# A decoder layer on one core: rows turned by DMA, the first two products in turn, weights laid out by the host

## Chip, core and metric

The kernel runs on one core of a Trainium2 chip. The metric is the device time of one launch in microseconds (us), the median over several runs. The core has five instruction streams that run side by side and wait for one another through semaphores: PE or TensorE (matrix products), DVE (VectorE), ACT (ScalarE), POOL (GpSimd) and SP (SyncE, which here only issues DMA transfers). ACT issues a few DMAs as well. The inputs lie in HBM, the working data in SBUF (128 partitions), and products accumulate in PSUM.

## What is computed

One layer of a hybrid decoder on 256 tokens of width 2048, in fp32, batch 1:

```python
hn = rmsnorm(h, norm_mix_w)
q, k, v, g_ret, xr, yr, g_a, g_b = split(hn @ w_in)
ret_out = silu(g_ret) * head_groupnorm(chunkwise_retention(rotary(q), rotary(k), v))
rnn_out = gelu(yr) * rg_lru(causal_dwconv(xr))
merged = sigmoid(g_a) * (ret_out @ w_proj_ret) + sigmoid(g_b) * (rnn_out @ w_proj_rnn)
h = h + merged @ w_mix_out
h = h + memory_cross_attention(rmsnorm(h), rmsnorm(mem), xa_w_q, xa_w_k, xa_w_v, xa_w_o)
h = h + conv_gated_ffn(rmsnorm(h), ffn_w_up, ffn_w_down)
out = rmsnorm(h, final_norm_w)
```

`mem` has 256 tokens as well. The weights are 2048 x 14336 (`w_in`), seven of 2048 x 2048, 2048 x 11264 (`ffn_w_up`) and 5632 x 2048 (`ffn_w_down`): nearly all of the 388 MB that are read.

## The kernel before

**Products.** Every large product is cut into blocks of 512 output columns (`BW`) and walks its inner dimension in chunks of four 128-row tiles (`KC`). A chunk's weights are a tile `raw` of 1 MB. For precision each weight is split into a rounded part `hi` (an ACT cast, L214) and a rest `lo` (a DVE subtraction, L215), and so is the other operand (tiles named `s`, `v`). A product is then three partial products, without the lo-by-lo term.

`gemm_n` (L279 to 281) leaves tokens on the partitions: three matmuls of 512 columns for each 128-row tile and each half of the tokens, 96 for a block of 16 tiles. `gemm_t` (L269) leaves features on the partitions: for each tile and each of four 128-column groups one matmul of 512 columns (both parts of `s` against `hi`) and one of 256 (the rounded part against `lo`), 64 pairs for a block.

**The stream of weights.** `plan` lists the products in order, `stream` their chunks. `prefetch` issues the load of a chunk on SP's queue and then the casts and subtractions; it runs two chunks ahead (`AHEAD`). There are three `raw` buffers and six half-chunk buffers each for `hi` and `lo`, so a cast waits until TensorE has read the half-chunk three chunks back. A weight chunk lies in HBM as 512 rows of the matrix, so each partition gets four rows of 2 KB.

**Order.** A scheduler orders each engine's instructions ahead of time; each engine then runs its own list in that order. `later(n, fn)` puts work `n + 1` chunks behind the current one.

**Rows that must be turned.** The result of `gemm_n` has tokens on the partitions, but the next product needs features there. `transposed` (L309) turns 128 x 128 squares on TensorE, against the identity `cid`, into PSUM tiles `sm`, four squares in a group. It is used for the heads' outputs (`rc`), for the merged rows (`m`, `turn_merged`), and for the residual rows after `w_mix_out` and after `xa_w_o` (`nat`, `turn`). A turned pair is split into parts by `split_pair` or `split_cols` (ACT, then DVE; L330, L353, L354). For the block that ends last the product behind it is already running: its last chunk of rows needs the turned pairs.

**Start.** The first product is Q's first block. Its pieces of `w_in` and of the transposed input `x_t` are issued in turn on SP (`Pairs`, `xs`), then V's first block, then K's. The row sums of squares of x (`rms`, L429) are eight ACT instructions in one go, on tiles `nat` loaded on ACT's queue; they give a scale per token, `rs0`. `spread_tokens` lays such a scale out along the free dimension: a diagonal on DVE (L379) and two products with ones (L380), then an ACT copy into `rsb`.

**Memory attention.** `xa_w_k` works on the memory tokens, whose pairs `ms` are split from loads `xt<-in_mem_t` on the way; two of the eight are made ahead.

Of the kernel before, what the change touches and what calls it, by code (L numbers as in the profile page):

```python
# [11 lines left out]
I32 = mybir.dt.int32  # L12
AF = mybir.ActivationFunctionType
# [3 lines left out]
P = 128  # L17
# [20 lines left out]
FF_PARTS = [4, 4, 3]  # L38

# [23 lines left out]

@with_exitstack
def hybrid_layer(
# [5 lines left out]
    w_in: bass.AP,  # L71
    rg_w_a: bass.AP,
    rg_w_x: bass.AP,
    w_proj_ret: bass.AP,
    w_proj_rnn: bass.AP,
    w_mix_out: bass.AP,
    xa_w_q: bass.AP,
    xa_w_k: bass.AP,
    xa_w_v: bass.AP,
    xa_w_o: bass.AP,  # L80
    ffn_w_up: bass.AP,
    ffn_w_down: bass.AP,
    final_norm_w: bass.AP,
    consts: bass.AP,
# [64 lines left out]
    w0 = w_in[0]  # L149
    plan = []  # L150
    for g in range(2):
        for c in (O_Q, O_K):
            plan += [(w0, 0, NT, c + g * BW), (w0, 0, NT, O_V + g * 1024 + (c == O_K) * BW)]
        plan += [(w0, 0, NT, O_G + g * 1024 + b * BW) for b in range(2)]
    for b in range(4):
        plan += [(w0, 0, NT, c + b * BW) for c in (O_XR, O_YR)]
    for c, w in ((O_GB, w_proj_rnn[0]), (O_GA, w_proj_ret[0])):
        for b in range(4):
            plan += [(w0, 0, NT, c + b * BW), (w, 0, NT, b * BW)]
    plan += [(w_mix_out[0], 0, NT, b * BW) for b in range(4)]  # L160
    plan += [(w, 0, NT, b * BW) for b in range(4) for w in (xa_w_k[0], xa_w_q[0])]
    plan += [(w, 0, NT, b * BW) for w in (xa_w_v[0], xa_w_o[0]) for b in range(4)]
    b0 = 0
    for nb_ in FF_PARTS:
        for b in range(b0, b0 + nb_):
            plan += [(ffn_w_up[0], 0, NT, c + b * BW) for c in (0, FF)]
        plan += [(ffn_w_down[0], b0 * BW, 4 * nb_, b * BW) for b in range(4)]
        b0 += nb_
    stream = [(w, row + k * P, c) for w, row, nk, c in plan for k in range(0, nk, KC)]
# [11 lines left out]

    def prefetch(n):
        while len(ahead) < n and taken[0] < len(stream):
            w, row, c = stream[taken[0]]
            taken[0] += 1
            raw = wp.tile([P, KC, BW], F32, tag="raw", bufs=RAW_BUFS, name=nm("raw"))
            src = w[row : row + KC * P, c : c + BW].rearrange("(k p) n -> p k n", p=P)
            first = taken[0] == 1
            if taken[0] <= 4:
                xs.load(2 * taken[0] - 1)  # L190
            for a, b in ((0, 1), (1, 2), (2, 4)) if first else ((0, 2), (2, 4)) if taken[0] <= 3 else ((0, 4),):
                sp.dma_start(out=raw[:, a:b, :], in_=src[:, a:b, :])
                if first and a == 0:
                    sp.dma_start(out=xs.rest[0], in_=xs.rest[1])
                elif first and a == 1 or a == 0 and taken[0] <= 4:
                    xs.load(2 * taken[0])
            if taken[0] == 5:
# [3 lines left out]
            if taken[0] == 7:  # L201
                sp.dma_start(out=pf.rearrange("p a n -> p (a n)"), in_=by_feature[:, P + 80 :])
            parts = []
            for k in range(0, KC, KH):
                if taken[0] <= 4:
                    xs[2 * (taken[0] - 1) + k // KH]
                hi = wp.tile([P, KH, BW], F32R, tag="hi", bufs=PART_BUFS, name=nm("hi"))
                lo = wp.tile([P, KH, BW], F32R, tag="lo", bufs=PART_BUFS, name=nm("lo"))
                for cs in (slice(k, k + 1), slice(k + 1, k + 2)) if first and k == 0 else (slice(k, k + KH),):
                    ds = slice(cs.start - k, cs.stop - k)  # L210
                    if first and k == 0:
                        dve.tensor_copy(hi[:, ds], raw[:, cs, :])
                    else:
                        act.copy(hi[:, ds], raw[:, cs, :])  # L214
                    dve.tensor_tensor(  # L215
                        out=lo[:, ds], in0=raw[:, cs, :], in1=hi[:, ds].bitcast(F32), op=ALU.subtract
                    )
                parts.append((hi, lo))
            ahead.append(((row, c), parts))
            if taken[0] >= 4:  # L220
                load_x(min(4, 2 * (taken[0] - 3)))
# [7 lines left out]
    def chunks(nk, w, row, c):  # L229

        w_, row_, nk_, c_ = plan[gemms[0]]
        assert (row_, nk_, c_) == (row, nk, c) and w_.tensor is w.tensor, (gemms[0], row, nk, c)
        gemms[0] += 1
        for k in range(0, nk, KC):
# [4 lines left out]
            yield k, parts  # L239
# [6 lines left out]
    def gemm_t(w, row, st, nk, col):  # L246
# [4 lines left out]
        for k0, parts in chunks(nk, w, row, col):  # L251
            last = k0 + KC >= nk
            tiles = [(kk, j) for j in range(2) for kk in range(KC)]
            if first and k0 == 0:
                runs = [[(t, pr, kk, j) for t in (0, 1)] for pr in range(2) for kk in range(KC) for j in range(2)]
# [5 lines left out]
            for i, run in enumerate(runs):  # L261
# [10 lines left out]
                if i + 1 == len(runs) // 2 and not last:  # L272
                    st[(k0 + KC) // 2 + 1]
        return accs
# [8 lines left out]
    def gemm_n(w, row, st, nk, col):  # L283

        a = acc()
        for k0, parts in chunks(nk, w, row, col):
            for tt in range(2):
                for kk in range(KC):
# [3 lines left out]
        return a  # L292
# [10 lines left out]
    def transposed(rows):  # L303

        for k in range(0, rows.shape[2], 2 * P):
# [6 lines left out]
            yield t  # L312

# [59 lines left out]

    def spread_tokens(r):

        diag = tmp("diag")
        bc = small((P, S))
        for tt in range(2):
            dve.tensor_scalar_mul(diag[:, 0, tt * P : (tt + 1) * P], ident, r[:, tt : tt + 1])  # L379
            pe.matmul(  # L380
                bc[:, tt * P : (tt + 1) * P], ones, diag[:, 0, tt * P : (tt + 1) * P], start=True, stop=True
            )
        act.copy(rsb, bc)
# [9 lines left out]
    class Pairs(list):  # L393
        def __init__(self, src, wcol):
            self.src, self.wcol, self.raw = src, wcol, []
# [14 lines left out]
        def __getitem__(self, i):  # L410
            while len(self) <= i:
                k2 = len(self)
                self.load(min(NT // 2, k2 + 2))
# [3 lines left out]
    xs = Pairs(x_t, p_mix)  # L417
    qjoin = [joined(t, "q") for t in gemm_t(w0, 0, xs, NT, O_Q)]
# [4 lines left out]
    def rms(rows, pin=False):  # L423

        ss = sp_.tile([P, 2, 4], F32, tag="ss0", name=nm("ss"))
        for c in range(4):
            for tt in range(2):
                junk = tp.tile([P, BW], F32, tag="tmp", name=nm("junk"))
                i = act.activation(junk, rows[c][:, tt, :], AF.Square, accum_out=ss[:, tt, c : c + 1])  # L429
                if pin:  # L430
                    tc.keep_in_program_order(i)
        var = sp_.tile([P, 2], F32, tag="var", name=nm("var"))
        dve.tensor_reduce(out=var, in_=ss, axis=AX.X, op=ALU.add)
        return rsqrt_small(var, 2, 1.0 / D, EPS)

    rs0 = rms(xin, pin=True)
    dve.tensor_scalar_mul(half_rs0, rs0, 0.5)
    rsb = cp.tile([P, S], F32, name="rsb")
# [19 lines left out]
    def tables():  # L458
        spread_tokens(rs0)
# [16 lines left out]
    later(1, tables)  # L476
# [81 lines left out]
    for g in range(2):  # L558
        dec = big([P, 4, S], s="dec")
        vs, turned = [], []  # L560
        for b, o in enumerate((O_Q, O_K)):
            a = qjoin if g == b == 0 else [joined(t, "q") for t in gemm_t(w0, 0, xs, NT, o + g * BW)]
            if b == 0:
# [6 lines left out]
            v = gemm_n(w0, 0, xs, NT, O_V + g * 1024 + b * BW)  # L570
# [5 lines left out]
        for b in range(2):  # L576
            a = gemm_n(w0, 0, xs, NT, O_G + g * 1024 + b * BW)
# [71 lines left out]
    for b in range(4):  # L649
# [4 lines left out]
        for pr, a in enumerate(gemm_t(w0, 0, xs, NT, O_XR + b * BW)):  # L654
# [11 lines left out]
        for pr, a in enumerate(gemm_t(w0, 0, xs, NT, O_YR + b * BW)):  # L666
# [12 lines left out]
    def gated(c0, w, st, b, o):  # L679

        a = gemm_n(w0, 0, xs, NT, c0 + b * BW)
# [13 lines left out]
    mb = [gated(O_GB, w_proj_rnn[0], rnn, b, big([P, 2, BW], s="mb")) for b in range(4)]  # L695
    for b in range(4):
        m = gated(O_GA, w_proj_ret[0], ret, b, big([P, 2, BW], s="m"))
# [7 lines left out]
    ms = Pairs(mem_t, p_mem)  # L705

    def residual(w, st, out, wcol, steps=None):

        ss = sp_.tile([P, 2, 4], F32, tag="ss0", name=nm("ss"))
        for b in range(4):  # L710
# [9 lines left out]
    def turn(b, pr, out, wcol):  # L720
        for t in transposed(hrow[b][:, :, pr * S : (pr + 1) * S]):
            out.append(split_cols(t, lambda j: wcol(4 * b + 2 * pr + j)))
# [9 lines left out]
    def rstd_rows(ss):  # L732
        var = sp_.tile([P, 2], F32, tag="var", name=nm("var"))
        dve.tensor_reduce(out=var, in_=ss, axis=AX.X, op=ALU.add)
        return rsqrt_small(var, 2, 1.0 / D, EPS)

    rsms = []

    def memory_steps(b):
        if b == 1:  # L740
            rsms.append(rms(mnat))
            later(3, lambda: spread_tokens(rsms[0]))
# [6 lines left out]
    ss1 = residual(w_mix_out[0], merged, h1s, p_xa, memory_steps)  # L749
# [41 lines left out]
    for b in range(XH):  # L791
        ks = []
        for a in gemm_t(xa_w_k[0], 0, ms, NT, b * BW):
# [159 lines left out]
```

## Time and profile before

| | us |
|---|---|
| median of 3 runs (2048.63 to 2052.51) | 2050.64 |
| the profiled execution | 2048.89 |
| its span, first to last instruction | 2047.1 |
| TensorE busy / DVE / ACT | 2035.0 / 1309.3 / 1045.3 |
| weight loads of 1 MB, issue to landing, median | 4.9 to 5.1 |

The span is what the profile sees of the execution; the rest of the 2048.89 lies around it. Busy time is the union of an engine's instructions. Matmuls are pipelined, so a single one shows 0.39 us in the timeline while the next one starts 0.23 us after it; what a piece of work costs TensorE is read from the starts. In a timeline row the columns are the start, the duration, engine, line, operation, tiles (out<-in), shape and count, and in brackets the idle time of the engine before it and what ended that. In a row of groups the count is followed by busy time and mean duration in ns, then by the idle time before them. In a row of waits stand the total, the number of times and the longest. A row of DMA issues ends with the size of one and the median time from issue to landing.

### The profile page before, as it was taken

The numbers are of one execution on the slowest core, as the hardware profiler recorded it, in microseconds if no ns is written. First come the engines' busy times: TensorE is split into PE (matmuls) and PEld (weight loads), VectorE is DVE, ScalarE is ACT, GpSimd is POOL, SyncE is SP. The second block draws the span as 40 slices with busy tenths as digits, with TensorE's granted clock in tenths as the row PEclk, the third lists the DMA queues.
The fourth block names the chain that finished last, engine by engine and source line by source line (L and its number), as shares of the span: only waits on it lengthen the run. The fifth ranks groups of instructions, "written<-read, shape, count | busy, mean of one in ns | idle before, by whom it ended". The sixth has DMA issues, their size and how long they took to land.

```text
span 2047.1 us, 26196 instructions
## 1 busy us (share of the span) xinstructions
PE 2035.0 (99%) x10508; PEld 1746.4 (85%) x10508; DVE 1309.3 (64%) x1630; ACT 1045.3 (51%) x1357; POOL 7.7 (0%) x12
## 2 busy tenths in 40 slices
PE   9999999999999999999999999999999999999998
PEld 7888888888888888888888888888888888888887
DVE  6858758888444544566555555577764777656774
ACT  6545447677434444555444544455543555435553
POOL 0000000000000000000000000000000000000000
PEclk9999999999999999999999999999999999999999
DMA  9664554555655555766555555555555555655563
GB/s 327 210 211 152 199 191 160 175 178 180 209 187 196 192 185 190 261 210 211 176 178 176 174 173 176 179 180 198 193 185 205 184 188 185 202 189 182 189 216 114
DMA packets 200682, 392.25 MB, mean 192 GB/s; under 512 B 7024, under 2 KB 11760, under 8 KB 200560
## 3 DMA queue, kind: packets, MB, share of 16 engines
q1 hardware_dynamic: 199040, 387.95, 55.7%
q10 hardware_dynamic: 1520, 2.63, 0.4%
q8 instruction: 82, 1.34, 0.3%
q14 instruction: 40, 0.33, 0.0%
HBM read 388.46 MB, written 2.10 MB: 191 GB/s over the span
## 4 chain that ended last, share of the span: by engine, by line
PE 79%; DVE 0%; ACT 0%; issue 0%; POOLq 0%; DVEq 0%
PE acc L269 35%; PE acc L280 14%; PE acc L281 14%; PE acc L279 14%; PE sm L297 1%; PE sm L309 1%; PE sm L623 0%; DVE xr L640 0%; PE sm L783 0%; ACT hi L214 0%; ACT nat L878 0%; DVE lo L215 0%; ACT c L319 0%; PE sm L380 0%; ACT s L330 0%
## 5 line engine op out<-in xcount | busy, mean ns | idle before, releaser
L215 DVE TENSOR_TENSOR lo<-raw,hi 128x1024 fp32r<-128x1024 f32 (+1 forms) x713 | 860.3, 1222 | 608.4 <-ACT hi L214 562.4
L214 ACT CAST hi<-raw 128x1024 fp32r<-128x1024 f32 x711 | 736.2, 1052 | 718.3 <-PE acc L280 455.0
L269 PE MATMUL acc<-s,hi 128*128 128x512 f32 x2688 | 639.0, 391 | 2.5 <-ACT hi L214 1.9
L279 PE MATMUL acc<-hi,s 128*128 128x512 f32 (+1 forms) x1528 | 591.9, 387 | 0.0
L281 PE MATMUL acc<-lo,s 128*128 128x512 f32 (+1 forms) x1528 | 590.1, 386 | 0.0
L280 PE MATMUL acc<-hi,s 128*128 128x512 f32 (+1 forms) x1528 | 590.0, 386 | 0.0
L269 PEld LDWEIGHTS acc<-s,hi 128*128 128x128 f32 x2688 | 496.5, 188 | 101.7 <-ACT hi L214 2.7
L269 PEld LDWEIGHTS acc<-s,lo 128*128 128x128 f32 x2688 | 342.7, 191 | 11.8 <-DVE lo L215 1.1
L269 PE MATMUL acc<-s,lo 128*128 128x256 f32 x2688 | 350.4, 283 | 0.5 <-DVE lo L215 0.5
L281 PEld LDWEIGHTS acc<-lo,s 128*128 128x128 f32 x1528 | 287.1, 188 | 57.9
L280 PEld LDWEIGHTS acc<-hi,s 128*128 128x128 f32 x1528 | 287.2, 188 | 57.1 <-DVE s L331 0.4
L279 PEld LDWEIGHTS acc<-hi,s 128*128 128x128 f32 x1528 | 287.2, 188 | 56.6
L319 ACT COPY c<-acc 128x512 f32<-128x512 f32 x84 | 48.6, 581 | 111.8 <-PE acc L269 111.8
L320 DVE TENSOR_TENSOR uz<-acc,c 128x512 f32<-128x512 f32 x44 | 30.3, 688 | 27.4 <-ACT c L319 27.4
L835 DVE SCALAR_TENSOR_TENSOR fg<-uz,pf,fg 128x255 f32<-128x255 f32 (+1 forms) x88 | 39.2, 479 | 0.0
L835 DVE SCALAR_TENSOR_TENSOR fv<-uz,pf,fv 128x255 f32<-128x255 f32 (+1 forms) x88 | 38.4, 480 | 0.0
L353 ACT ACTIVATE s<-sm,pb 128x256 fp32r<-128x256 f32 x48 | 21.9, 471 | 17.7 <-DVE s L354 16.7
L443 DVE TENSOR_TENSOR uz<-uz,rsb 128x512 f32<-128x512 f32 x44 | 30.3, 689 | 0.7
L330 ACT ACTIVATE s<-fo 128x512 fp32r<-128x512 f32 x22 | 13.9, 632 | 26.7 <-DVE fo L904 26.7
L833 ACT ACTIVATE fv<-uz,pf 128x256 f32<-128x256 f32 x44 | 25.3, 600 | 2.5 <-DVE uz L443 2.5
L354 DVE SCALAR_TENSOR_TENSOR s<-sm,pb,s 128x256 fp32r<-128x256 f32 x48 | 22.4, 481 | 5.1 <-ACT s L353 5.1
L833 ACT ACTIVATE fg<-uz,pf 128x256 f32<-128x256 f32 x44 | 25.3, 599 | 0.0
(167 smaller groups left out, 731.0 us busy)
## 6 DMA issues: line engine op xcount, KB each, us to landing
raw<-in_w_in SPq DMA_DIRECT2D x109, 1024.0 KB, 5.0
raw<-in_ffn_w_up SPq DMA_DIRECT2D x88, 1024.0 KB, 4.9
raw<-in_ffn_w_down SPq DMA_DIRECT2D x44, 1024.0 KB, 5.1
raw<-in_w_proj_rnn SPq DMA_DIRECT2D x16, 1024.0 KB, 5.1
raw<-in_w_proj_ret SPq DMA_DIRECT2D x16, 1024.0 KB, 5.1
raw<-in_w_mix_out SPq DMA_DIRECT2D x16, 1024.0 KB, 5.1
raw<-in_xa_w_k SPq DMA_DIRECT2D x16, 1024.0 KB, 5.1
raw<-in_xa_w_q SPq DMA_DIRECT2D x16, 1024.0 KB, 5.1
```

Of the source, the lines that this page charges most:

```text
L214: act.copy(hi[:, ds], raw[:, cs, :])
L215: dve.tensor_tensor(out=lo[:, ds], in0=raw[:, cs, :], in1=hi[:, ds].bitcast(F32), op=ALU.subtract)
L269: pe.matmul(a, part, sx, start=k == 0 and t == 0, stop=k == nk - 1 and t == 0, skip_group_check=True)
L279: pe.matmul(o, h, hi, start=start, stop=False)
L280: pe.matmul(o, l, hi, start=False, stop=False)
L281: pe.matmul(o, h, lo, start=False, stop=stop)
L319: act.copy(c, a[:, :, S:BW])
L320: dve.tensor_tensor(out=o, in0=a[:, :, 0:S], in1=c, op=ALU.add)
L354: dve.scalar_tensor_tensor(out=t[:, j, S:BW], in0=src[:, j, :], scalar=wcol(j), in1=t[:, j, 0:S].bitcast(F32), op0=ALU.mult, op1=ALU.subtract,
L443: dve.tensor_tensor(out=z, in0=z, in1=rsb2, op=ALU.mult)
L833: act.activation(y, z[:, j, :], AF.Identity, scale=pf[:, 2, t : t + 1], bias=pf[:, 3, t : t + 1])
L835: dve.scalar_tensor_tensor(out=y[:, s:S], in0=z[:, j, 0 : S - s], scalar=pf[:, 2 - s, t : t + 1], in1=y[:, s:S], op0=ALU.mult, op1=ALU.add,)
```

## The change

There are five edits.

1. The merged rows and the residual rows are no longer turned on TensorE. ACT copies a block of rows into two planes of 16-bit halves, SP issues two transposing DMAs, one for each half of the tokens, and two chunks later ACT joins the halves into a tile `f`, which is split as before. The heads' outputs and the attention's probabilities are still turned on TensorE.
2. Q's first block and V's first block are computed in turn, in pieces of 2, 2, 4, 4 and 4 tiles.
3. All weights are handed over in one array `wall`, laid out by the host in the order of the stream, so that each partition of a chunk reads one row of 8 KB.
4. The eight squares of x are made as two groups of four, each ahead of the casts of one later chunk.
5. `spread_tokens` builds the diagonal at once and returns a function for the products and the copy.

```diff
+EARLY = [2, 2, 4, 4, 4]
...
+def weight_stream():
+    out = [
+        [(w, row + k * P, n, c) for k, n in pieces(i, nk)]
+        for i, (w, row, nk, c) in enumerate(weight_plan())
+    ]
+    out[:2] = [[one for pair in zip(*out[:2]) for one in pair]]
+    return [one for chunks in out for one in chunks]
...
+def weights_in_order(inputs):
+    out = []
+    for name, row, n, c in weight_stream():
+        w = np.asarray(inputs[name])[0][row : row + n * P, c : c + BW].reshape(n, P, BW)
+        out.append(w.transpose(1, 0, 2).reshape(-1))
+    return np.concatenate(out)
...
-            w, row, c = stream[taken[0]]
+            i = taken[0]
+            name, row, nk, c = stream[i]
             taken[0] += 1
+            size = nk * P * BW
+            src = wall[at[0] : at[0] + size].rearrange("(p k n) -> p k n", p=P, k=nk)
...
+            if i in (8, 9):
+                for b in (2 * i - 16, 2 * i - 15):
+                    sum_squares(xin[b], ss0, b, pin=True)
...
+    def by_dma(rows, then):
+        planes = big([P, 2, 2, BW], U16, s="pl")
+        turned_ = big([P, 2, 4, S], U16, s="pt")
+        words = rows.bitcast(U16).rearrange("p t (n h) -> p h t n", h=2)
+        for h in range(2):
+            act.copy(planes[:, :, h, :], words[:, h])
+        for tt in range(2):
+            sp.dma_start_transpose(
+                out=turned_.rearrange("p h f s -> p (h f) s")[:, :, tt * P : (tt + 1) * P],
+                in_=planes[:, tt].rearrange("p h n -> p (h n)"),
+            )
+        def join():
+            f = big([P, 4, S], s="f")
+            halves_ = f.bitcast(U16).rearrange("p f (s h) -> p h f s", h=2)
+            for h in range(2):
+                act.copy(halves_[:, h], turned_[:, h])
+            then(f)
+        later(1, join)
...
     def spread_tokens(r):
-        diag = tmp("diag")
-        bc = small((P, S))
+        diag = tp.tile([P, S], F32, tag="tr", bufs=2, name=nm("diag"))
         for tt in range(2):
-            dve.tensor_scalar_mul(diag[:, 0, tt * P : (tt + 1) * P], ident, r[:, tt : tt + 1])
-            pe.matmul(
-                bc[:, tt * P : (tt + 1) * P], ones, diag[:, 0, tt * P : (tt + 1) * P], start=True, stop=True
-            )
-        act.copy(rsb, bc)
+            dve.tensor_scalar_mul(diag[:, tt * P : (tt + 1) * P], ident, r[:, tt : tt + 1])
+        def products():
+            bc = small((P, S))
+            for tt in range(2):
+                cs = slice(tt * P, (tt + 1) * P)
+                pe.matmul(bc[:, cs], ones, diag[:, cs], start=True, stop=True)
+            act.copy(rsb, bc)
+        return products
...
-    xs = Pairs(x_t, p_mix)
-    qjoin = [joined(t, "q") for t in gemm_t(w0, 0, xs, NT, O_Q)]
+    xs = Pairs(x_t, p_mix, 1)
+    q_steps = steps_t("w_in", 0, xs, NT, O_Q)
+    v_steps = steps_n("w_in", 0, xs, NT, O_V)
+    for _ in EARLY[1:]:
+        next(q_steps)
+        next(v_steps)
...
-    def turn_merged(m, pr):
-        for t in transposed(m[:, :, pr * S : (pr + 1) * S]):
-            merged.append(split_pair(t, 0.5))
+    def turn_merged(f):
+        for pr in range(2):
+            merged.append(split_pair(f[:, 2 * pr : 2 * pr + 2, :], 0.5))
...
         dve.tensor_add(m, m, mb[b])
-        for pr in range(2):
-            later(pr, lambda m=m, pr=pr: turn_merged(m, pr))
+        by_dma(m, turn_merged)
...
             squares(h, ss, b)
-            for pr in range(2):
-                later(pr, lambda b=b, pr=pr: turn(b, pr, out, wcol))
+            by_dma(hrow[b], lambda f, b=b: turn(f, b, out, wcol))
```

`steps_t` and `steps_n` are `gemm_t` and `gemm_n` written as generators that stop after each chunk; `gemm_t` and `gemm_n` now run them to the end.

More of the change, by code (lines that the diff above doesn't have):

```diff
@@ L70, in hybrid_layer @@
     positions: bass.AP,
-    w_in: bass.AP,
     rg_w_a: bass.AP,
     rg_w_x: bass.AP,
[L74 to L82, printed above, removed]
     final_norm_w: bass.AP,
+    wall: bass.AP,
     consts: bass.AP,
@@ L146, in hybrid_layer @@
         pe.matmul(warm[:, 0, 0:P], ones, ones, start=True, stop=True)
[L149 to L169, printed above, removed]
+    plan = weight_plan()
+    stream = weight_stream()
     ahead, taken, gemms = [], [0], [0]
@@ L244, in chunks, with ended, steps_t @@
                 fn()
-    def gemm_t(w, row, st, nk, col):
+    def ended(steps):
+        for a in steps:
+            pass
+        return a
+    def steps_t(w, row, st, nk, col):
         accs = [acc(), acc()]
@@ L271, in gemm_t @@
                     )
-                if i + 1 == len(runs) // 2 and not last:
-                    st[(k0 + KC) // 2 + 1]
-        return accs
+                if i + 1 == len(runs) // 2 and not last and not first and isinstance(st, Pairs):
+                    st[(k0 + n) // 2 + 1]
+            yield accs
+    def gemm_t(*args):
+        return ended(steps_t(*args))
     def products_n(o, sx, hi, lo, tt, start, stop):
@@ L474, in tables @@
         dve.tensor_tensor(out=cos, in0=cos, in1=rsb, op=ALU.mult)
-    later(1, tables)
+    qjoin = [joined(t, "q") for t in next(q_steps)]
+    assert next(q_steps, None) is None
+    later(0, tables)
     def rotated(qs_):
@@ L792, in hybrid_layer @@
         ks = []
-        for a in gemm_t(xa_w_k[0], 0, ms, NT, b * BW):
+        for a in gemm_t("xa_w_k", 0, ms, NT, b * BW):
             z = joined(a, "kz")
```

187 lines of the change are left out of this document (109 added, 78 removed).

## The prediction

> **What bounds the kernel.** I read the page's busy times first, then the list of waits on TensorE.
>
> ```profile
> span 2047.1 us, 26196 instructions
> ...
> PE 2035.0 (99%) x10508; PEld 1746.4 (85%) x10508; DVE 1309.3 (64%) x1630; ACT 1045.3 (51%) x1357; POOL 7.7 (0%) x12
> ```
> ```profile
> PE acc L269 <- ACT hi L214: 1.9, 1, 1.9
> PE warm L146 <- DVE mhalf L141: 1.1, 1, 1.1
> PE sm L380 <- DVE diag L379: 0.6, 1, 0.6
> ```
>
> TensorE is idle for 12 us of 2047: before the first product, for two or three waits, and behind the last matmul (2039.4, so 7.7 us). Only two things can shorten this: less TensorE work, or a better start. Faster weights, DVE or ACT give nothing. Next the timeline of TensorE around one group of turning transposes, and the group rows:
>
> ```profile
> 887.01 0.39 PE L281 MATMUL acc<-lo,s 128*128 128x512 f32 x1
> 887.24 0.60 PE L309 MATMUL sm<-cid,nat 128*128 128x128 f32 x4
> 887.59 0.48 PE L279 MATMUL acc<-hi,s 128*128 128x512 f32 x1
> 887.91 0.40 PE L280 MATMUL acc<-hi,s 128*128 128x512 f32 x1
> 888.14 0.40 PE L281 MATMUL acc<-lo,s 128*128 128x512 f32 x1
> ```
> ```profile
> L309 PE MATMUL sm<-cid,nat 128*128 128x128 f32 x64 | 9.6, 272 | 0.0
> L309 PE MATMUL sm<-cid,m 128*128 128x128 f32 x32 | 4.8, 272 | 0.0
> ```
>
> Matmuls start every 0.227 us (512 wide) or 0.120 (256 wide). L281 at 887.01 should be followed by the next L281 at 887.69; it starts at 888.14. So four transposes cost 0.45 us.
>
> **The change, part by part.**
>
> *Transposes off TensorE.* 32 of `m` and 64 of `nat` are 24 groups: 24 x 0.45 = 10.8 us less on the path. The other transposes stay, and nothing is added to TensorE.
>
> *Start.* Timelines of TensorE and ACT:
>
> ```profile
> 8.07 0.91 ACT L353 ACTIVATE s<-xt,pa 128x256 fp32r<-128x256 f32 x2 [3.36 <-DMA xt<-in_x_t]
> 9.42 1.05 ACT L214 CAST hi<-raw 128x1024 fp32r<-128x1024 f32 x1 [0.44 <-DMA raw<-in_w_in]
> 10.52 0.74 PE L269 MATMUL acc<-s,hi 128*128 128x512 f32 x2 [1.95 <-ACT hi L214]
> 11.78 0.39 PE L269 MATMUL acc<-s,lo 128*128 128x256 f32 x1 [0.53 <-DVE lo L215]
> ```
>
> Q's first product runs from 4.75 to 30.94 (first L279), 26.2 us; its 64 pairs at 0.347 are 22.2: 4.0 lost, waiting for DMA, which by stretches of 2 us is full from 8 us on (374 to 404 GB/s). By queue order 1024 KB had landed at 8.05 and 1536 KB at 9.4. In the change the first piece of V lies within the first 1024 KB, so V starts at 8.05 + 0.5 (half an ACT cast) = 8.6 instead of standing until 10.52. V's first 12 matmuls take 2.7, to 11.3; the next Q piece closes 2048 KB, 10.8 at 385 GB/s, cast by 11.8. After that two k-blocks of Q and V need 1.25 MB per 5.5 us, 233 GB/s. Lost: 8.6 - 7.5 + 0.5 = 1.6, gain 2.4; bounds 0 (no better) and 4.0 (all).
>
> *Token scales.* The diagonal is built ahead of its two products, and the eight squares stand as two groups of four ahead of the casts of two later chunks. The L380 wait goes, 0.71 us with its sequencer time. The groups (four at 0.63 each) wait for `nat`, issued on ACT's queue and 8 to 13 us on the way, so there by about 29 and 36; the casts behind them are for products at 39 and 45. If that cover goes, each late us is a us.
>
> *Host-laid weights.* One 8 KB row per partition instead of four of 2 KB. Zero: a 1 MB load lands in 5.0 us, a chunk takes TensorE 5.45, and three buffers run ahead. If the cover went, it could only be a gain.
>
> *The DMA turn.* Per block of 512 columns: two ACT copies to 16-bit planes, two transposing DMAs of 256 KB on SP, two ACT copies back. Copies: nearest row 1.05 us for 128x1024, lower bound 0.58 (128x512 f32), upper 2.1 (two passes); I take 1.05. ACT gains 12 x 4.2 = 50 us of work and is half idle. No row has a transposing DMA. Call X the time from the last plane copy to the landing of both DMAs. The rows:
>
> ```profile
> out<-nat SPq DMA_DIRECT2D x6, 256.0 KB, 2.3
> ...
> cid<-in_consts SPq DMA_DIRECT2D x1, 65.0 KB, 8.3
> pa<-in_by_feature SPq DMA_DIRECT2D x1, 56.0 KB, 8.0
> pb<-in_by_feature SPq DMA_DIRECT2D x1, 40.0 KB, 7.5
> pa<-in_by_feature ACTq DMA_DIRECT2D x1, 8.0 KB, 2.5
> ```
>
> Lowest: two 2.3 us transfers issued 0.45 apart, 2.8. `cid`, `pa`, `pb` were issued at 16.18, 16.73, 17.48, so landed at 24.5, 24.7, 25.0: 128 small rows add 0.22 to 0.24 us whatever their length (320 to 520 B), 27.5 ns for each row on one of 16 engines. The source is read by runs of 128 two-byte elements, 2048 runs of 256 B: 128 x 27.5 ns = 3.5, plus issue 0.9, plus landing 2.3: X = 7. If the destination is written in runs of 16 elements (16384), 28 + 3: X = 31. If sixteen 128x128 squares go one after another, each a lone 2.5 us transfer: X = 39.5. I take 7: both sides have long contiguous runs.
>
> What waits: SP stands at the turn until the planes are made, with the next weight load behind it; that load's buffer comes free within about 2 us of the same moment, so nothing. ACT stands at the join copy, with the hi casts of the coming chunks behind it, and TensorE behind those. With T the end of the product that made the rows, planes end at T+7.3 for `m` (one hi cast goes first, its buffer free at T+4.1) and T+5.3 for the residual rows (add 1.2, squares 1.3, planes 2.1). The casts behind the join are mostly for the product at T+21.8 (96 x 0.227). Counting back casts, splits (0.45 and 0.6) and the join's 2.1, no stall while X is under: `m` blocks 0 to 2: 12; block 3: 12.7 (TensorE does a chunk and a bit of the next block first); `w_mix_out` rows 0 to 2: 18, 17, 10; `xa_w_o` rows 0 to 2: 14; row 3: 8, since the FFN wants it at T+16.4.
>
> One place stalls anyway, after the last `w_mix_out` block:
>
> ```profile
> 927.58 1.05 ACT L214 CAST hi<-raw 128x1024 fp32r<-128x1024 f32 x1 [0.61 <-PE acc L281]
> 929.39 0.63 ACT L730 ACTIVATE junk<-nat 128x512 f32<-128x512 f32 x1 [0.76 <-DVE nat L714]
> ...
> 932.58 0.91 ACT L353 ACTIVATE s<-xt,pb 128x256 fp32r<-128x256 f32 x2
> ```
>
> `xa_w_k`'s second chunk needs memory pairs (`s<-xt,pb`) at T+5.45 (two transposes' worth later here). With planes and one cast ahead of them they come at T+6.35 to 8.15: 1.9 us late. The last two pairs stand behind the join: 0.9 more at X = 7, and each us of X beyond 7 is a us. I add 2.8.
>
> Sum: -10.8 - 2.4 - 0.7 + 2.8 = -11.1: span 2036.0. The profiled execution took 2048.9, 1.8 over its span; the median of the runs is 2050.6. **Forecast 2050.6 - 11.1 = 2039.5.** Own range: all of the start and no late pairs, 2035; no start gain and copies at 2.1 (about 2 more at that place and the FFN row), 2044; with 2 us of spread between runs, 2033 to 2046.
>
> **Rivals.**
>
> *The turn is a little late*, X of 10 to 14 (transposes queue behind a weight load in flight, 5.0 us). At 12: 5 at the memory pairs, 4 at row 3 of `xa_w_o`, 2 at row 2 of `w_mix_out`: +11, so 2050.5, no change. For: those loads are on the same queue. Against: the load just ahead of the turn is issued some 5 us before it.
>
> *The turn is late everywhere; slower.* Mechanism: small runs, ACT held at the join. It decides from X = 12. At X = 31: 3x19 + 18 + 13 + 14 + 21 + 24 + 3x17 + 23 = 221, time 2260. For: the cost per small row above. Against: it needs both sides cut to 32 B.
>
> *Squares one after another; slower.* At X = 39.5 the same sum is 323: 2363. Against: plain DMAs overlap over 16 engines (share 1.05). By the Trainium skill, page "VectorE: DVE Perf Modes", section "The three transpose paths", a 128x128 two-byte transpose takes 1309 ns by DMA against 390 ns on TensorE; sixteen in a row would make X 20.9, stalls 100 and the time 2140, an estimate from that page. The trace prices TensorE's at 0.45/4 = 0.11 us for fp32, so the page's comparison does not settle this one; no run here yet shows the DMA's.
>
> *It does less than it says:* the start is bound by the first 1.5 MB whatever the order, 2042; inside my range.
>
> **Chances.** Forecast 0.62 (2033 to 2046); a little late 0.12 (2046 to 2056); late everywhere 0.13; one after another 0.08; another stall of a few us in a product whose order on ACT I have not priced 0.05. A measurement of this kernel tells 0.2% from no change, about 4 us. Faster 0.64, within 0.2% 0.09, slower 0.27. 2031 to 2060 holds the first two, most of the last and the near end of the late ones.
>
> **What would show it.** Right: no `cid,m` and `cid,nat` transposes; TensorE starting V near 8.6; join copies on ACT with no idle time ended by the DMA beyond 3 us; TensorE idle in all about 12 to 14 us. Wrong: TensorE waits on `hi` spread over the gated, `w_mix_out` and `xa_w_o` stages (X too large); landings of the turned planes over 12 us; plane copies far from 1.05 us; a wait at `xa_w_k` that is absent or far over 3 us.

## The result, and the profile after

The changed kernel took 2039.24 us (median of 4 runs, 2038.36 to 2042.19), the kernel before 2050.58 (4 runs beside it, 2048.63 to 2052.51): ratio 0.9951, 95% interval 0.9938 to 0.9963. The forecast was 2039.5. The profiled execution took 2038.96 with a span of 2037.2; before it was 2047.1, so 9.9 us of the span went where 11.1 were forecast. That the median still lies within 0.3 us of the forecast is partly luck: between the medians 11.3 us went, and single runs of one kernel differ by up to 4 us.

In the changed kernel L309 and L322 to L324 are the matmuls that were L269 and L279 to L281, L248 and L249 the casts `hi` and `lo`, L422 the splits `s`, L367 the plane copies, L369 the turning DMAs and L378 the join copies. The page's busy times and the list of waits on TensorE (us in total, times, longest):

```profile
span 2037.2 us, 26091 instructions
...
PE 2024.4 (99%) x10412; PEld 1736.3 (85%) x10412; DVE 1306.7 (64%) x1631; ACT 1091.1 (54%) x1406; POOL 7.7 (0%) x12
```
```profile
PE acc L322 <- ACT hi L248: 1.6, 1, 1.6
PE warm L188 <- DVE mhalf L183: 1.1, 1, 1.1
PE acc L309 <- ACT s L422: 1.0, 1, 1.0
```

TensorE has 96 instructions and 10.6 us of busy time less. It is idle as long as before, 12 to 13 us: the 1.9 us wait for the first casts and the 0.6 for the diagonal are gone, but a wait of 1.6 for a cast and one of 1.0 for a split have come. The timeline of TensorE shows the first, which ends 9 us later than the one it replaces (19.81 against 10.52):

```profile
17.51 0.74 PE L309 MATMUL acc<-s,lo 128*128 128x256 f32 x4 [0.38 <-DVE lo L249]
19.81 0.50 PE L322 MATMUL acc<-hi,s 128*128 128x512 f32 x1 [1.56 <-ACT hi L248]
```

The windows of the same stretch (PE, PEld, DVE, ACT and POOL busy, granted clock, DMA share, GB/s) show weights coming slowly ahead of it, 193 GB/s at 12 to 14 us where 404 were moved before (first the row of before, then the changed kernel):

```profile
12.00:14.00 2.00, 2.00 (x13) 1.78 (x13) 2.00 (x4) 1.83 (x4) 0.00 (x0) 1.00 1.05 404
```
```profile
10.00:12.00 2.00, 2.00 (x10) 1.41 (x9) 1.11 (x3) 1.57 (x2) 0.00 (x0) 1.00 0.90 299
12.00:14.00 2.00, 2.00 (x14) 1.74 (x13) 1.96 (x3) 1.34 (x3) 0.00 (x0) 1.00 0.83 193
14.00:16.00 2.00, 2.00 (x12) 1.70 (x11) 0.58 (x2) 0.85 (x1) 0.00 (x0) 1.00 1.00 322
16.00:18.00 2.00, 1.62 (x9) 1.08 (x8) 1.77 (x3) 1.98 (x4) 0.00 (x0) 1.00 0.99 371
18.00:20.00 2.00, 0.43 (x4) 0.23 (x3) 1.59 (x3) 1.12 (x3) 0.00 (x0) 1.00 1.04 398
```

The second wait is the one that was forecast at `xa_w_k`. The timeline of ACT there:

```profile
923.12 1.98 ACT L367 COPY pl<-nat 128x1024 uint16<-128x1024 uint16 x2
925.01 1.04 ACT L248 CAST hi<-raw 128x1024 fp32r<-128x1024 f32 x1
925.96 1.70 ACT L422 ACTIVATE s<-xt,pb 128x256 fp32r<-128x256 f32 x4
927.57 1.03 ACT L248 CAST hi<-raw 128x1024 fp32r<-128x1024 f32 x1
928.50 1.71 ACT L422 ACTIVATE s<-xt,pb 128x256 fp32r<-128x256 f32 x4
930.33 2.57 ACT L378 COPY f<-pt 128x1024 uint16<-128x1024 uint16 x2
```

Planes and one cast stand ahead of the memory pairs (`s<-xt,pb`), the join behind them: the order that the prediction gave. And the turn itself, in the view of the tile `pt` (ns: shortest, median, longest):

```profile
L369 SPq DMA_TRANSPOSE pt<-pl x24: 1237/1314/3272, 708.7 to 1305.1; - x24
L378 ACT COPY f<-pt x24: 1337/1347/1362, 713.5 to 1310.0; 128x1024 uint16<-128x1024 uint16 x24
...
DMA to landing us min/median/max: 3.1/3.7/5.6
```

From the last plane copy to the second landing, X was 4.5 to 6.5 us over the twelve blocks. ACT stood idle for a join six times, 10.1 us in all, and no wait on TensorE's list stands behind one of them.

For the experiments I sum what TensorE loses against its steady spacing of matmul starts (0.227, 0.120, 0.109 us for 512, 256 and 128 columns), by stages. Two stages matter: the first 50 us, called the start, and 900 to 950 us (`xa_w_k`'s first chunks). Lost before: 6.8 (0.7 of it L380's wait) and 0.2; after: 6.1 and 1.8. The first matmul of K's first block, the product that follows Q's and V's, starts at 54.04 before and at 53.35 after; below, K stands for this moment.

### The profile page after: what moved, and what is told of

The parts are those of the page before. It is cut to its first block, busy times and chain, and to the rows that moved or that the text cites. A ratio compares the mean times of both kernels' runs of the same rounds, so it can differ in the third digit from the quotient of the medians.

```text
span 2037.2 us, 26091 instructions
## 1 busy us (share of the span) xinstructions
PE 2024.4 (99%) x10412; PEld 1736.3 (85%) x10412; DVE 1306.7 (64%) x1631; ACT 1091.1 (54%) x1406; POOL 7.7 (0%) x12
## 2 busy tenths in 40 slices
DMA packets 90121, 398.53 MB, mean 196 GB/s; under 512 B 32400, under 2 KB 37136, under 8 KB 44944
## 4 chain that ended last, share of the span: by engine, by line
PE 79%; ACT 0%; DVE 0%; issue 0%; POOLq 0%; DVEq 0%
PE acc L309 35%; PE acc L323 14%; PE acc L322 14%; PE acc L324 14%; PE sm L343 1%; PE sm L710 0%; ACT hi L248 0%; DVE xr L727 0%; PE sm L866 0%; ACT pl L367 0%; ACT nat L961 0%; DVE lo L249 0%; ACT c L388 0%; PE sm L455 0%; ACT s L399 0%
## 5 line engine op out<-in xcount | busy, mean ns | idle before, releaser
L249 DVE TENSOR_TENSOR lo<-raw,hi 128x1024 fp32r<-128x1024 f32 (+1 forms) x714 | 858.1, 1220 | 603.6 <-ACT hi L248 562.9
L248 ACT CAST hi<-raw 128x1024 fp32r<-128x1024 f32 (+1 forms) x712 | 732.4, 1048 | 670.7 <-PE acc L323 401.6
L309 PE MATMUL acc<-s,hi 128*128 128x512 f32 x2688 | 637.1, 391 | 0.6 <-ACT c L388 0.4
L322 PE MATMUL acc<-hi,s 128*128 128x512 f32 (+1 forms) x1528 | 590.1, 386 | 1.6 <-ACT hi L248 1.6
L324 PE MATMUL acc<-lo,s 128*128 128x512 f32 (+1 forms) x1528 | 589.8, 386 | 0.0
L309 PEld LDWEIGHTS acc<-s,hi 128*128 128x128 f32 x2688 | 496.5, 188 | 99.8 <-ACT hi L248 0.8
L309 PEld LDWEIGHTS acc<-s,lo 128*128 128x128 f32 x2688 | 342.2, 191 | 13.8 <-DVE lo L249 1.7
L309 PE MATMUL acc<-s,lo 128*128 128x256 f32 x2688 | 350.0, 284 | 1.6 <-ACT s L422 1.0
L322 PEld LDWEIGHTS acc<-hi,s 128*128 128x128 f32 x1528 | 287.1, 188 | 59.3 <-ACT hi L248 2.1
L324 PEld LDWEIGHTS acc<-lo,s 128*128 128x128 f32 x1528 | 287.0, 188 | 58.5 <-DVE lo L249 0.7
L378 ACT COPY f<-pt 128x1024 uint16<-128x1024 uint16 x24 | 30.8, 1350 | 10.2 <-DMA pt<-pl 10.1
L748 DVE SCALAR_TENSOR_TENSOR xr<-xz,pa,xr 128x255 f32<-128x255 f32 (+2 forms) x48 | 20.0, 480 | 0.0
```

The lines of the kernel that those rows point to most:

```text
L249: dve.tensor_tensor(out=lo[:, ds], in0=raw[:, cs, :], in1=hi[:, ds].bitcast(F32), op=ALU.subtract)
L309: pe.matmul(a, part, sx, start=k == 0 and t == 0, stop=k == nk - 1 and t == 0, skip_group_check=True)
L322: pe.matmul(o, h, hi, start=start, stop=False)
L324: pe.matmul(o, h, lo, start=False, stop=stop)
L378: act.copy(halves_[:, h], turned_[:, h])
```

## Experiments

**1. The turn undone.**

```diff
-        by_dma(m, turn_merged)
+        for pr in range(2):
+            later(pr, lambda m=m, pr=pr: turn_merged(m, pr))
...
-            by_dma(hrow[b], lambda f, b=b: turn(f, b, out, wcol))
+            for pr in range(2):
+                later(pr, lambda b=b, pr=pr: turn(b, pr, out, wcol))
```

> The changed kernel (span 2037.2 us) with one part undone: the 96 turning transposes of m and nat are back on TensorE, no planes, no turning DMAs, no join copies; all else as changed. Theory: the turn is worth 24 groups x 0.45 = 10.8 us of TensorE and costs only the 1.0 to 1.8 us stall at xa_w_k's second chunk, so the span is 2037.2 + 10.8 - 1.4 = 2046.6 (2046 to 2047), TensorE busy 10.6 to 10.8 us more, and the wait of L309 on ACT s L422 is gone. Rival: the start and the token scales carry part of the gain and the turn less (hidden losses spread over the gated stages); then the span is 2044.5 or less.

Span 2046.7; median 2048.73 of 10 runs (2047.58 to 2050.20), ratio to before 0.9995 (0.9985 to 1.0005). The page's busy line has TensorE's 96 transposes back:

```profile
PE 2034.9 (99%) x10508; PEld 1745.3 (85%) x10508; DVE 1309.6 (64%) x1631; ACT 1043.9 (51%) x1358; POOL 7.7 (0%) x12
```

The wait on `s` is gone and the loss at 900 to 950 is 0.1. So the turn carries nearly the whole gain, and all the rest of the change cannot be told from nothing. The last matmul starts 9.56 us later than in the changed kernel, whose start lost 0.2 and whose stage at 900 to 950 lost 1.7 more: the transposes are worth 9.56 + 1.9 = 11.4 us, 0.48 for a group of four.

**2. Q's product whole, then V, as before.** The core of the edit; pieces, squares and buffers go back with it:

```diff
-    sizes = EARLY if i < 2 else [KC] * (nk // KC)
+    sizes = [KC] * (nk // KC)
...
-    q_steps = steps_t("w_in", 0, xs, NT, O_Q)
-    v_steps = steps_n("w_in", 0, xs, NT, O_V)
-    for _ in EARLY[1:]:
-        next(q_steps)
-        next(v_steps)
+    qjoin = [joined(t, "q") for t in gemm_t("w_in", 0, xs, NT, O_Q)]
```

> The changed kernel with the start undone: Q's product runs whole, then V's first block, pieces, raw buffers and squares as they were before; transposing DMAs, host-laid weights and the early diagonal kept. Theory: taking Q and V in turn gained nothing, since what V gains at 8 us is lost again at 18 to 20 us, so the span stays at 2037.2 within 0.5 and the first matmul of K starts within 0.7 of 53.4 us. Rival (the prediction's term): the interleave is worth 2.4 us, span 2039.6 and K 2.4 us later, at 55.8.

Span 2036.2, K at 52.60, the start's loss 5.4 against 6.1. The term of 2.4 is refuted. Since profiled runs of one and the same start differ by more than this, the kernel was also timed:

> The kernel of the start undone once more (Q whole, then V, raw buffers, pieces and squares as before; all else as changed), timed in five rounds, since the loss at the start differed by 1.4 us between looks at one and the same start. Theory: taking Q and V in turn is worth nothing; median 2039.2 within 1, like the changed kernel's 2039.24. Rival of the prediction: it is worth 2.4, median 2041.6.

Median 2038.28 of 5 runs (2037.92 to 2039.88), ratio 0.9945 (0.9931 to 0.9958), where the changed kernel has 0.9951 (0.9938 to 0.9963). Its profiled run had span 2038.1 and K at 54.44, with 7.2 lost; the windows show why that is more than 5.4:

```profile
12.00:14.00 2.00, 2.00 (x9) 1.71 (x8) 1.53 (x3) 1.90 (x4) 0.00 (x0) 0.53 1.03 412
14.00:16.00 2.00, 2.00 (x9) 1.73 (x8) 2.00 (x4) 1.90 (x4) 0.00 (x0) 0.61 1.05 410
```

The granted clock fell to 0.53 and 0.61 for 4 us, which costs 2 x 0.47 + 2 x 0.39 = 1.7; without it the loss is 5.5. Taking Q and V in turn, as it stands with its pieces, buffers and squares, is worth nothing.

**3. Why not: buffers, or the order?** First the buffers.

```diff
-            raw = wp.tile([P, KC, BW], F32, tag="raw", bufs=RAW_BUFS, name=nm("raw"))
+            if nk == KH:
+                raw = big([P, KH, BW], s="raw")
+            else:
+                raw = wp.tile([P, KC, BW], F32, tag="raw", bufs=RAW_BUFS, name=nm("raw"))
```

> The changed kernel with more buffers at the start: the half-size raw tiles of the first chunks (512 KB) come from the big pool instead of the three raw buffers, so that SyncE need not stand for a raw buffer. Theory A (buffers): in the changed kernel the loads pause at 6.7 to 12.6 us because the three raw buffers hold half-size tiles; here DMA runs at 375 GB/s or more through 8 to 16 us, the 1.6 us wait at 18 to 20 us is gone, K starts 1.5 to 2.5 us earlier (51 to 52) and the span falls to 2034.7 to 2035.7. Theory B (bandwidth): DMA was full anyway; K within 0.4 us of 53.4. Theory C (order): a product of Q's and V's next chunk is put ahead of the one that is ready; the wait at 18 to 20 us stays.

Span 2035.2, K at 51.37, 4.1 lost at the start, no wait over 0.3 us at 18 us. The windows:

```profile
10.00:12.00 2.00, 1.97 (x9) 1.33 (x8) 1.10 (x3) 1.67 (x4) 0.00 (x0) 1.00 0.99 395
12.00:14.00 2.00, 2.00 (x11) 1.65 (x11) 2.00 (x4) 1.68 (x4) 0.00 (x0) 1.00 1.05 422
14.00:16.00 2.00, 2.00 (x13) 1.75 (x12) 1.94 (x2) 1.90 (x4) 0.00 (x0) 1.00 1.02 416
16.00:18.00 2.00, 2.00 (x11) 1.55 (x9) 2.00 (x4) 1.70 (x2) 0.00 (x0) 1.00 1.06 418
18.00:20.00 2.00, 1.73 (x13) 1.64 (x13) 1.82 (x3) 1.77 (x4) 0.00 (x0) 1.00 1.02 415
```

DMA moves 395 to 422 GB/s where the changed kernel had 299, 193 and 322, and K and the span lie where theory A put them. With three raw buffers, each holding only half of its size, SyncE stood before loads that the DMA engines had room for. Its issues show it, in the changed kernel and then here (loads in a row are one line, with the start of the first):

```profile
4.02 3.03 SPq L223 DMA_DIRECT2D raw<-in_wall  x2
7.10 0.43 SPq L501 DMA_DIRECT2D xt<-in_x_t  x1
9.51 0.33 SPq L223 DMA_DIRECT2D raw<-in_wall  x1
```
```profile
4.97 1.47 SPq L226 DMA_DIRECT2D raw<-in_wall  x2
6.49 0.84 SPq L504 DMA_DIRECT2D xt<-in_x_t  x1
7.37 3.58 SPq L226 DMA_DIRECT2D raw<-in_wall  x3
```

What it is worth is less sure than the cause. All eight profiled runs that take Q and V in turn with three raw buffers (the changed kernel and experiments 1, 3, 4, 5, 6 and 7) fell to 188 to 277 GB/s at 12 to 14 us, and lost 4.8 to 6.6 at the start without the clock's part, 5.9 in the mean. The two with more room, this one and the kernel of experiment 8, moved 422 and 412 GB/s and lost 4.1 and 4.9. That is some 1.4 us, not the 2.0 of this one pair of runs.

Then the order, with the matmuls of Q's first product held in program order:

```diff
-                    pe.matmul(
+                    m = pe.matmul(
...
+                    if first:
+                        tc.keep_in_program_order(m)
```

> The changed kernel with the matmuls of Q's first product held in the order of the program, so that the scheduler cannot place V's matmuls of the next chunk among them; nothing else is changed. Theory C (order): the 1.6 us wait at 18 to 20 us is there because V's matmuls of the chunk not yet cast stand ahead of Q's that are ready; here it shrinks under 0.5, K starts 1 to 1.5 us earlier (52 to 52.4) and the span falls to 2036. Theory A (buffers, loads late): the weights come no earlier, so the idle time is moved, not removed: K within 0.4 us of 53.4 and the span within 0.5 of 2037.2.

Span 2039.3, K at 55.52, two waits (0.8 and 1.6 us) at 17.6 and 18.9 us, and a granted clock of 0.72 at 20 to 24 and 0.85 at 24 to 28 us (1.7 us). The order is not the cause; idle time was only moved, as theory A had it. The span is 2.1 over the changed kernel's, 1.7 of it the clock; the 0.4 that is left is within the 0.5 that theory A allowed.

**4. The layout of the weights.** Rows of 2 KB again, in the changed kernel and in the kernel of experiment 2:

```diff
-        out.append(w.transpose(1, 0, 2).reshape(-1))
+        out.append(w.reshape(-1))
...
-            src = wall[at[0] : at[0] + size].rearrange("(p k n) -> p k n", p=P, k=nk)
+            src = wall[at[0] : at[0] + size].rearrange("(k p n) -> p k n", p=P, k=nk)
```

> The changed kernel with the weights laid so that a chunk's load reads rows of 2 KB again, four per partition, instead of one of 8 KB; order and sizes of the loads are the same. Theory (the prediction's step): nothing waits for the weights' landing but the start; DMA packets go back from 90,000 to near 200,000, the first matmul of K stays within 0.4 us of 53.4 and the span within 0.5 of 2037.2. Rival: at the start, where TensorE does wait for weights, 8 KB rows move 400 to 420 GB/s and 2 KB rows 375 to 400; then K comes 0.7 to 1.7 us later and the span is 2038 to 2039.

> The start of before (Q's first product whole, then V; pieces, raw buffers and squares as before) and rows of 2 KB, with the DMA turn and the early diagonal kept: the kernel with 8 KB rows in this order had K's first matmul at 52.6 and span 2036.2. Theory (layout pays at the start): DMA falls from 412-423 to 375-405 GB/s in the 10 to 20 us windows and K comes 0.7 to 1.5 us later, span 2037 to 2037.7. Rival (layout is worth nothing; the 0.9 us by which that kernel led the changed one is the order alone): K at 52.6 and span 2036.2 within 0.4.

In the changed kernel packets rise from 90121 to 226057 and K starts at 52.98, 5.7 lost: no worse, as forecast. The span is 2037.9, from another place: 2.9 lost at 900 to 950, because the last turn of `w_mix_out` took X = 6.7 there instead of 5.2 and the last two memory pairs, behind its join, came late by 1.1 us. With Q whole the span is 2039.2 and K at 54.88, 7.7 lost, but the clock was at 0.92, 0.50 and 0.73 from 10 to 16 us (1.7 us); the remaining 6.0 is 0.5 over the 5.4 and 5.5 with 8 KB rows, and like the 6.1 of before without L380's wait. At 10 to 20 us DMA moved 386 to 408 GB/s, against 411 to 423 and 399 to 440 in the two profiled runs of experiment 2. An effect of half a microsecond is at the edge of what these runs tell; I leave it open.

**5. The turn made longer**, each transposing DMA issued three times into the same tile:

```diff
-        for tt in range(2):
-            sp.dma_start_transpose(
+        for _ in range(3):
+            for tt in range(2):
+                sp.dma_start_transpose(
```

> The changed kernel with every transposing DMA issued three times, into the same tile (72 instead of 24), so that the last landing comes later; nothing is computed differently. X, the time from the last plane copy to the last landing, was 4.5 to 6.5 us; if the six issues take 1.3 us each it is about 11, if each repeat waits for the one before, about 15. The prediction's slacks (12 for m, 18, 17, 10 and 5 for the w_mix_out rows, 14 and 8 for the xa_w_o rows, each late us a us of TensorE) give: at X = 11, 1 at row 2 of w_mix_out, 4 to 6 at the memory pairs, 3 at row 3 of xa_w_o, span +8 to +10, 2046; at X = 15, 11 for m, 5, 8 to 10, 3 and 7, span +34, 2071. Rival (the scheduler's order leaves far more room than was counted): the span grows by under 4 us.

X became 13.1 to 18.3 and the span 2080.5, +43.3, against +34 forecast for X = 15. The waits on TensorE, and from ACT's timeline the join of the first block of `m` and a later group of casts:

```profile
PE acc L309 <- DVE s L424: 15.6, 1, 15.6
PE acc L309 <- ACT s L423: 10.7, 2, 7.9
PE sm L456 <- DVE diag L450: 4.9, 1, 4.9
```
```profile
725.32 2.56 ACT L379 COPY f<-pt 128x1024 uint16<-128x1024 uint16 x2 [2.18 <-DMA pt<-pl]
...
865.03 2.00 ACT L248 CAST hi<-raw 128x1024 fp32r<-128x1024 f32 x2 [8.81 <-DMA raw<-in_wall]
```

Blocks 0 to 2 of `m`, at X = 16.6, 18.0 and 18.0, lost nothing: their slack is at least 18, not 12. At 864 to 880 us 3.5 us were lost, 2 of them (at 865) in another way than counted: SyncE, standing for the repeats, issued the weight loads late, and ACT waited 8.8 us for them. The large stalls are where they were priced: 15.7 us at 924.8, where `xa_w_k`'s pairs stand behind planes and join, and 3 more at 960; 5.1 and 8.1 with the late rows of `xa_w_o` (for the last, the slack of 8 prices 18.3 - 8 = 10.3). These stalls come to 35.4 us. Most of the rest is the clock: when TensorE started again after the stalls of 15.7, 3.0, 5.1 and 8.1 us, the granted clock was 0.50 in windows of 2 us (942 to 944, 966 to 968, 1340 to 1342, 1361 to 1367) and back at 1.00 within 4 to 8 us, which costs some 8 us in all. So the total hides a miss: by the prediction's slacks these X would have cost 54 us, 17 of them at `m`, where nothing was lost.

**6. The place at 925 us.** First four of the eight memory pairs ahead of the last block's planes:

```diff
             later(1, lambda: ms[1])
+            later(2, lambda: ms[2])
+            later(3, lambda: ms[3])
```

> The changed kernel with the last two pairs of the memory chunks made in two further steps of w_mix_out's last block instead of behind the join (two lines added), so that ACT has no pairs left to make when xa_w_k begins. Theory: the 1.0 to 1.2 us wait of L309 on ACT s at 925 us is gone and nothing takes its place, span 2035.7 to 2036.1. Rival: the wait is for ACT's order of planes and casts ahead of the pairs and only changes its tile; span within 0.4 of 2037.2.

Span 2035.3, which looks like the theory, but for the wrong reason: this run lost only 4.8 at a start that is the changed kernel's own. At 900 to 950 it still lost 1.4 of 1.8. The wait at 925 is gone, and one came at 936, in ACT's and TensorE's timelines:

```profile
930.83 2.58 ACT L378 COPY f<-pt 128x1024 uint16<-128x1024 uint16 x2 [0.51 <-DMA pt<-pl]
933.27 1.03 ACT L248 CAST hi<-raw 128x1024 fp32r<-128x1024 f32 x1
934.21 1.70 ACT L422 ACTIVATE s<-f,pb 128x256 fp32r<-128x256 f32 x4
935.82 1.69 ACT L422 ACTIVATE s<-xt,pb 128x256 fp32r<-128x256 f32 x4
```
```profile
936.36 0.39 PE L309 MATMUL acc<-s,lo 128*128 128x256 f32 x1 [0.95 <-ACT s L422]
```

The last pairs stand behind the join: the second half of the prediction's stall. Two things brought it out, and these runs do not part them: the first wait no longer held TensorE back, and X at this block was 6.7 in this run, 5.2 in the changed kernel. Then six pairs, from block 2 on:

```diff
-        if b == 3:
+        if b == 2:
             ms.load(2)
-            later(0, lambda: ms[0])
-            later(1, lambda: ms[1])
+            later(2, lambda: ms[0])
+            later(3, lambda: ms[1])
+        if b == 3:
+            for i in range(4):
+                later(i, lambda i=i: ms[2 + i])
```

> The changed kernel with six of the eight memory pairs made within the steps of w_mix_out's last two blocks (with four of them, the wait at 925 us went and one of 0.95 us came at 936, for the last pairs, which stood on ACT behind the join copies). Theory: with six made ahead, the last two stand ahead of the join copies and TensorE waits for nothing between 900 and 960 us; the loss there falls from 1.8 to under 0.3, span 2035.5 (2034.5 to 2036.2, the start varying by 0.7 either way). Rival: the pairs, made earlier, delay the hi casts of w_mix_out's last blocks, and a wait of L322 on ACT hi comes in their place; loss there over 1.

Neither: 2.7 lost, span 2038.4 (its start lost 6.5). ACT's timeline:

```profile
932.12 2.56 ACT L378 COPY f<-pt 128x1024 uint16<-128x1024 uint16 x2 [3.13 <-DMA pt<-pl]
934.54 1.04 ACT L248 CAST hi<-raw 128x1024 fp32r<-128x1024 f32 x1
935.47 1.71 ACT L422 ACTIVATE s<-f,pb 128x256 fp32r<-128x256 f32 x4
937.09 1.03 ACT L248 CAST hi<-raw 128x1024 fp32r<-128x1024 f32 x1
938.02 1.70 ACT L422 ACTIVATE s<-xt,pb 128x256 fp32r<-128x256 f32 x4
```

I had put the last two pairs ahead of the join; they are written behind it and stay there, while ACT stands idle 3.1 us for the landing. The early pairs also delayed the rows, a form of the rival: their splits stand on DVE ahead of the block's add (L800), which ran at 922.61 instead of 920.63 though TensorE was only 0.3 us later, so that the planes came 1.6 us later by the same count. It is the join that has to move.

**7. The heads turned by DMA too.**

```diff
-        for t in transposed(raw):
-            ret.append(split_cols(t, lambda j: half_gn[:, g * 8 + hh * 2 + j : g * 8 + hh * 2 + j + 1]))
+        def split(t):
+            ret.append(split_cols(t, lambda j: half_gn[:, g * 8 + hh * 2 + j : g * 8 + hh * 2 + j + 1]))
+
+        by_dma(raw, split, DV)
```

> The changed kernel with the heads' 32 remaining transposes also turned by DMA, in 8 blocks of 256 columns. Theory: 8 groups x 0.45 = 3.6 us less of TensorE and nothing else, since ACT and the queue have room in the retention stage as they had in the gated one: TensorE busy 2020.8, span 2033.6 (2033 to 2034.5). Rival: a turn takes 5 us and ACT 2.5 us per head, and the pairs of the last head of a group are wanted before; TensorE then waits on ACT s in that product, and the span is 2036 or more.

Span 2037.2, with 7.5 lost at the start, 1.5 of it a granted clock of 0.62 at 20 to 24 us. Between 300 and 450 us TensorE loses 2.4 more than in the changed kernel, in waits where ACT and DVE are late (`lo` includes one of 0.8 at 18 us):

```profile
PE acc L309 <- DVE lo L249: 1.9, 2, 1.1
...
PE acc L309 <- ACT c L388: 0.9, 2, 0.7
PE sm L712 <- ACT ti L715: 0.5, 1, 0.5
```

So 3.6 gained, 2.4 given back: the rival's kind of loss, at other instructions than it named.

**8. What works, together**: more raw room, six pairs, the heads, and the join of `w_mix_out`'s last block behind the last two pairs:

```diff
-        later(1, join)
+        later(wait, join)
...
-            by_dma(hrow[b], lambda f, b=b: turn(f, b, out, wcol))
+            by_dma(hrow[b], lambda f, b=b: turn(f, b, out, wcol), wait=3 if steps and b == 3 else 1)
```

> The changed kernel with four edits together: the early half-size raw tiles from the big pool (alone: 2.0 us less lost at the start), six memory pairs made ahead and the join of w_mix_out's last block put behind the last two pairs, three steps later than before it (the two pairs stood behind that join in the looks before), and the heads turned by DMA (alone: 3.6 us less for TensorE, about 2.4 lost again between 345 and 412 us). Theory: the terms add, since they lie in different stages: 2.0 + 1.6 + 1.2 = 4.8 less, span 2032.4, median 2034.5 (2033 to 2036), no wait at 925 or 936. Rival: the wait of the memory pairs moves once more (as it did in the two looks before), to the join's late rows in xa_w_q; span 2034 or more, median 2036.

Median 2034.27 of 5 runs (2033.79 to 2034.76), ratio 0.9922 (0.9909 to 0.9936), span 2033.0. At 900 to 950 the loss is 0.0. All of TensorE's waits that the list shows:

```profile
PE acc L312 <- DVE lo L252: 1.1, 1, 1.1
PE warm L188 <- DVE mhalf L183: 1.1, 1, 1.1
PE acc L312 <- ACT c L391: 0.9, 2, 0.7
PE acc L325 <- ACT hi L251: 0.5, 2, 0.3
PE sm L715 <- ACT ti L718: 0.5, 1, 0.5
```

No wait on `s` is left. The start lost 4.9, 0.8 more than in experiment 3, enough for the 0.6 by which the span lies over the expected 2032.4. It beats both kernels.

## Why the prediction was right, and where it was not

*Transposes off TensorE:* right, and under-sized: 24 x 0.45 = 10.8 forecast, 11.4 measured by undoing them.

*Start:* wrong. -2.4 was forecast, 0 measured (K came 0.69 us earlier, all of it L380's term). V did start early, its first matmul at 7.96 us; the step that failed is "after that two k-blocks of Q and V need 1.25 MB per 5.5 us, 233 GB/s". It asked whether DMA could move the bytes, not whether SyncE had a buffer to issue them into: chunks of half size in three full-size buffers halve what can be under way. More buffers brought some 1.4, and DMA back to 412 and 422 GB/s.

*Token scales:* right, -0.7; the wait is gone.

*Host-laid weights at nothing:* held in the changed kernel, whose start was not better with them (6.1) than without (5.7).

*The turn.* X = 7 was forecast, 4.5 to 6.5 measured. Its parts were off in both directions: a transposing issue holds SyncE 1.31 us, where I took 0.45 from plain ones, while the landing came 3.7 us after the issue, where 128 x 27.5 ns + 2.3 = 5.8 was assumed. That X came near 7 is thus in part luck. Copies to planes took 1.04 (1.05 forecast), joins 1.35 (1.05). ACT's busy time rose by 45.8 us, 50 forecast, and was hidden. The slacks were safe: for `m` at least 18 instead of 12.

*The stall at `xa_w_k`:* right in place and mechanism, over-sized: 2.8 forecast, 1.6 measured (0.2 to 1.8). The 1.9 for late pairs was 1.6, a gap of 1.2 at 925 us and four of 0.1 right behind it. The 0.9 for the pairs behind the join was priced at X = 7; here X was 5.2 and it cost nothing. Where X was 6.7 (rows of 2 KB) that part came as 1.1.

*The sum:* -11.4 + 0 - 0.7 + 1.6 = -10.5, which is what the last matmul moved (2039.4 to 2028.9). The tail behind it grew from 7.7 to 8.2, a term that I did not have: the last outputs land after 2.8 us instead of 2.3. They do so in the kernel with the turn undone too, so it is not the turn; the cause stays open. Against the forecast of -11.1 the start's miss of 2.4 and the tail's 0.5 were made up, all but 1.1, by the stall's 1.2 and the transposes' 0.6. So the total was nearer than its terms, which is luck.

*Rivals:* the turn a little late, late everywhere, and square after square were all wrong; the tripled turn shows that an X of 13 to 18 does cost tens of microseconds, though not where `m` was priced; X = 31 was not run. "The start is bound by the first 1.5 MB whatever the order, 2042" was right in that the start gains nothing, for another reason. The Trainium skill's 1309 ns for a 128x128 two-byte transpose by DMA (page "VectorE: DVE Perf Modes", section "The three transpose paths") does not add up square by square here: a 256 KB transfer of eight such squares, by the program's count, landed 3.1 to 5.6 us after its issue, where eight in a row would make 10.5, an estimate from that page's figure.

## What to carry to other kernels

When TensorE is busy all the time, work taken off it is worth its full duration, provided that the engines and queue that get it have slack where it lands; count that slack at the next product's first chunks, since there the late pairs were the only loss. When chunks are made smaller to start sooner, count the buffers as well as the bytes: a ring sized for large chunks holds less with small ones. And where one of two waits behind each other is removed, look for the second before claiming the sum: here it took the third edit.

## What the runs showed of the hardware

- A transposing DMA of 256 KB held SyncE for 1.24 to 3.27 us at its issue (median 1.31), where plain issues took 0.33 to 0.43 when nothing held them.
- It moved as 1056 packets under 512 B, 248 B each on average: the changed kernel has 32400 such packets with 24 of these DMAs, experiment 1 has 7056 with none, experiment 5 has 83088 with 72. The prediction's runs of 256 B, 1024 for each DMA, were about right.
- At the start of experiments 2 (timed), 3 (order), 4 (Q whole) and 7 the granted clock dropped for 4 to 8 us, somewhere between 10 and 28 us, to 0.50 at the lowest, soon after TensorE had stood idle for a microsecond or more; in other runs with the same start and the same idle time it stayed at 1.00. It costs 1.5 to 1.7 us, as much as several edits here are worth, and a single profiled run does not tell the two apart unless the windows are read. Behind each of the four stalls of 3.0 to 15.7 us in experiment 5 it dropped as well, to 0.50.
- One and the same start (after and experiments 1, 5, 6 and 7) lost 4.8 to 6.5 us once the clock's part is taken out; the span of a single profiled run is no evidence for an edit worth less than some 1.5 us, unless the stage it touches is read by itself.
